# An issue planner with refitted estimates, an early ScalarE table load and unpaired squares in a hybrid SSD/S5 layer

## The chip, the cores and the metric
The kernel runs on one core of one Trainium2 chip. The metric is the device time of one execution in microseconds (us), the median of three runs. TensorE (PE) multiplies matrices, VectorE (DVE), ScalarE (ACT) and GpSimd (POOL) work element by element, SyncE (SP) issues the transfers between main memory and the on-chip buffers.

## What is computed
One inference step of one layer, for 1024 frames of a new stream and 32 frames of a running one, in fp32:

```
xn = RMSNorm(x);  P = xn @ W_in  -> [z | xBC | dt | u]        (1024 -> z 512, xBC 1024, dt 8, u 512)
SSD: causal conv + SiLU on xBC, chunked scan over 8 heads, + D*x, gated by SiLU(z), grouped RMSNorm
S5:  32 groups of 16 channels, 64 complex states each, Re(C h) + D*u, GELU, per-group GLU
h = x + RMSNorm([ssd | s5] @ W_out)
[g | v] = causal_dwconv3(RMSNorm(h) @ W_up)                   (1024 -> 2 x 2816)
y = h + RMSNorm((gelu(g) * v) @ W_down)
```
The new states and the last rows of the convolutions are outputs too.

## The kernel before
The 1056 frames lie along the columns of every tile, the channels along the 128 partitions, and are worked in chunks of 512, 272 and 272 columns (0, 1, 2). Each fp32 operand of a large product is split into a high and a low half, and `mm` (L479) runs three products for one: xh·wh, xl·wh, xh·wl. ScalarE makes the high halves (`act`, L535), VectorE the low ones by subtraction: xl at L1045 for the input, L1662 for the second norm, wl at L713 for each 128x1024 weight block (`raw` is the block as it landed). The weights go by in an order written out at L687 and following: 16 blocks of W_in, W_out for each chunk, W_up, and W_down.

The head: `prologue` (L1033) loads the eight 128-channel pieces of a chunk's x into tiles `xst`, makes xh and xl of each, and hands the piece to `flush` (L1023), which squares it in place on ScalarE. For chunk 0 the squares of the pieces named in `pairs` are added to the square before on GpSimd (L1029). `norm_cols` (L675) then sums over the channels with matmuls of one column (`onec`, a column of ones), four 128-frame blocks for each remaining square; `rsq` (L597) computes the inverse root of the sums, beginning with `nrt` (L603) on VectorE, and `spread` makes the scale of all frames (`rbc`) by way of the tiles `scr` (L639 to L647). Products are computed from the unscaled x and multiplied by rbc when they are taken out of PSUM, at L758 (uext) in the S5 part and at L1721 (fext) in the feed-forward part.

S5 runs eight times over four groups each. In a run TensorE multiplies `ug` by `GT` into PSUM; VectorE scans; GpSimd and VectorE write `hq` (L1164 to L1168); TensorE multiplies hq by `W`; ScalarE and VectorE make `ge` (a GELU) of that; TensorE multiplies ge by the weight `gluw`. Between these steps stand matmuls of the input projection.

After W_out the first norm's result is put on x at L1659 (tile `o`, from the product's scaled `oacc`, eight times for chunk 0). At the end of chunk 0's feed-forward part VectorE adds up its output in `acc` (L1891, L1896) while chunk 1's W_up products run; dl (L1771) is the low half of a W_down block.

The order is set by the class `Plan`. The program's instructions are recorded, their dependencies found (`read`), each given a duration and a latency (`cost`), and a list scheduler (`schedule`) goes forward and backward over them, `rounds` times, with priorities from the pass before; the shortest planned end wins, and `apply` fixes each engine's order to it. A successor on another engine is ready when its predecessor ends plus a fixed hand-over. SP's transfer issues are part of the same order.

Of the kernel before, what the change touches and what calls it, by code (L numbers as in the profile page):

```python
# [9 lines left out]
F32 = mybir.dt.float32  # L10
# [37 lines left out]
           run3=0.5, uload=6.619, swap_pool=1, z_s5=1, ssd0=13.784, ssd1=0.0, ssd2=2.778, gate0=76.032, glu0=0.384, glu1=2.807, abufs=2,   # L48
           cvat='run7', tcat=1, late_at=2, nsq=1, fg=(), fp=((1, 3), (1, 3), (3,)), fch=(0, (0, 1), 2), pfin=0, q0=0, q1=0, q2=0, nb=0, 
           hv=(), av=(3,), post0=0.802, dn_at=((3, 0), (3, 1)), ob_at=22, sa=2, sb=1, y5b=0, cvb=2.11, msb=(1, 1, 2, 2, 2), pch0=(3,),   # L50
           pch1=(3,), pch2=(3, 4), pf=0, pb=500, pg=0, pn=500, pr=0, pairs=(1, 2, 3, 5, 6), cf=4, cb=1, cg=0, cf2=2, cb2=(0, 1), cg2=0, 
           pgt=500, p5at=1, ng=0, n12=(2, 0), cho=2, dtlag=112.5, ng2=1, pairs2=(1, 2, 3, 5, 6, 7))
WIN, WOUT, WUP, WDN = 0, 16, 24, 68
TAU = [7, 6, 5, 4, 3, 2, 1, 0, 1, 2, 3, 4, 5, 6, 7, 8]
# [127 lines left out]
class Plan:  # L182
# [61 lines left out]
    def read(self):  # L244
# [18 lines left out]
        for q, i in enumerate(ins):  # L263
            ia, oa = aps(i.ins), aps(i.outs)
            self.cost(q, i, ia, oa)
            for _, g in ia:
                self.pre[q].update(k for k, h in w.get(g[0], ()) if self.meet(g, h))
            for _, g in oa:
                for d in (w, r):
                    self.pre[q].update(k for k, h in d.get(g[0], ()) if self.meet(g, h))  # L270
            for _, g in oa:
                for d in (w, r):
                    d[g[0]] = [(k, h) for k, h in d.get(g[0], ()) if not self.holds(g, h)]
                w[g[0]].append((q, g))
                use.setdefault(g[0], []).append(q)
            for _, g in ia:
                r.setdefault(g[0], []).append((q, g))
                use.setdefault(g[0], []).append(q)
            if type(i).__name__ == "InstMatmult":
                if i.start_tensor_calc and oa[0][1][0] in closed:  # L280
                    self.pre[q].add(closed[oa[0][1][0]])
                closed[oa[0][1][0]] = q
            self.pre[q].discard(q)
# [58 lines left out]
    def cost(self, q, i, ia, oa):  # L342
        self.eng[q] = e = str(i.engine).split(".")[-1]
        kind = type(i).__name__
        n = max(self.free(a) for a, _ in ia + oa)
        if kind == "InstDMACopy":
            self.bytes[q] = 4 * int(np.prod([m for _, m in ia[0][0].ap]))
            self.dur[q], self.lat[q] = 0.06, 2.0
            return
        if kind == "InstMatmult":  # L350
            n, m = (self.free(a) for a, _ in ia[:2])
            if ia[0][0].dtype == F32R:
                d = max(0.43 * n + 6, 107 if m > 64 else 54)
            elif i.is_transpose:
                d = 112
            else:
                d = 2 * max(0.85 * n, 108) if m > 64 else 0.85 * n
            self.dur[q], self.lat[q] = d * 1e-3, 0.07
            return
        big = [a for a, _ in ia if self.free(a) > 1]  # L360
        ps = any(g[0].startswith(("ms", "pm")) for _, g in ia)
        if kind == "InstActivation":
            self.fset[q] = str(i.func).split(".")[-1]
            d = 0.19 + 0.00085 * n + 0.08 * (len(ia) > len(big))
        elif e == "Pool":
            self.shared[q] = len(big) > 1
            d = 0.21 + 0.00165 * n if len(big) > 1 else 0.12 + 0.0009 * n
        else:
            self.shared[q] = not ps and n > 8
            d = 0.15 + (0.00105 if ps or len(big) > 1 else 0.00053) * n  # L370
        self.dur[q] = d

    def schedule(self, rank, pre, suc, forward=True, gate=None):
# [5 lines left out]
        order = {e: [] for e in engs}  # L379
        lock = wire = 0.0  # L380
        lanes, cur = [0.0] * DMA_LANES, None
        for q in range(n):
            if not left[q]:
                heappush(wait[self.eng[q]], (0.0, q))
        parked, todo = [], n
        while todo:
# [16 lines left out]
            if e == "Activation" and forward and not gate:  # L403
                need = [ACTSET.get(self.fset[q], cur) for _, q in avail[e]]
                k = min(range(len(need)), key=lambda k: (avail[e][k][0] + (4.0 if need[k] != cur else 0.0), avail[e][k][1]))
                q = avail[e].pop(k)[1]
                heapify(avail[e])
                if need[k] != cur:
                    cur = need[k]
                    t += 1.3  # L410
            else:
                q = heappop(avail[e])[1]
            start[q] = s = t
            order[e].append(q)
            if self.bytes[q]:
# [16 lines left out]
                    heappush(wait[self.eng[x]], (t, x))  # L432
                parked = []
            for x in suc[q]:
                v = free[e] if self.eng[x] == e and not self.bytes[q] else end[q] + 0.06
                if v > ready[x]:
                    ready[x] = v
                left[x] -= 1
                if not left[x]:
                    heappush(wait[self.eng[x]], (ready[x], x))  # L440
        return max(end), order, start, end

    def apply(self, rounds=3):
        self.read()
        self.buffers()
        best = self.schedule(list(range(len(self.ins))), self.pre, self.suc)
# [12 lines left out]
def body(tc, xT, wt, wdt, vec, cst, dtp, hist4, hist3, h0ssd, s5p, s5bc, s5d, glu, glub,  # L459
# [200 lines left out]

    onec = con.tile([128, 1], F32, name="onec")
    G.memset(onec, 1.0)
    ones_r = con.tile([128, 128], F32R, name="ones_r")
    G.tensor_copy(ones_r, onec.to_broadcast([128, 128]))
    ones = ones_r.bitcast(F32)
# [1280 lines left out]
```

## Time and profile before

| | us |
|---|---|
| median of 3 runs (lowest, highest) | 1297.89 (1296.71, 1302.05) |
| the profiled execution, its own time | 1294.34 |
| its span, first to last instruction | 1292.4 |
| TensorE busy | 1225.8 |
| VectorE busy | 1035.2 |
| ScalarE busy | 574.5 |
| GpSimd busy | 397.7 |

The profile is one execution. Busy time is per engine and over the span; the granted clock is TensorE's, as a share of 2.4 GHz, so 0.50 is 1.2 GHz. In a timeline the bracket behind an instruction is the idle time of its engine before it and what ended it.

### The profile page before, as it was taken

How to read it: one execution, taken by the hardware profiler on the slowest of the kernel's cores; microseconds unless marked ns; L12 is line 12 of the kernel's file. 1: busy time of each engine (PE TensorE's matmuls, PEld its weight loads, DVE VectorE, ACT ScalarE, POOL GpSimd, SP SyncE). 2: the span in 40 equal slices, each digit the busy share in tenths (PEclk: the TensorE clock that was granted, in tenths of full speed). 3: DMA queues.
4: the chain of work that ended last, by engine and by line, in shares of the span. 5: the costliest groups of instructions: out<-in, count | busy, mean ns of one | idle time of the engine just before them, and what ended most of it. 6: DMA issues, size and time to landing. Idle time of an engine off the chain costs nothing.

```text
span 1292.4 us, 20981 instructions
## 1 busy us (share of the span) xinstructions
PE 1225.8 (95%) x7880; PEld 1105.6 (86%) x7880; DVE 1035.2 (80%) x1781; ACT 574.5 (44%) x979; POOL 397.7 (31%) x577
## 2 busy tenths in 40 slices
PE   6879999999998999999999999998999999999995
PEld 5768888888877888878977888887999999999994
DVE  7898887988988998987688977679577777777777
ACT  7236466554555555543444433353523333333243
POOL 5364554544146433211345110015111111111113
PEclk8989999999998999999999999999999999999997
DMA  7133323233434423234433333222323332222212
GB/s 220 57 96 99 96 76 114 79 106 93 124 105 164 152 91 99 81 104 137 153 99 123 122 99 98 95 85 82 117 81 98 99 98 82 95 86 83 82 52 70
DMA packets 66901, 132.14 MB, mean 102 GB/s; under 512 B 13936, under 2 KB 34800, under 8 KB 66800
## 3 DMA queue, kind: packets, MB, share of 16 engines
q1 hardware_dynamic: 66800, 130.81, 32.2%
q8 instruction: 62, 1.02, 0.3%
q14 instruction: 39, 0.32, 0.1%
HBM read 111.69 MB, written 15.81 MB: 99 GB/s over the span
## 4 chain that ended last, share of the span: by engine, by line
PE 79%; DVE 10%; POOL 3%; issue 3%; DMA 2%; ACT 1%; SPq 1%; DVEq 0%; ACTq 0%; POOLq 0%
PE pm L479 70%; PE ms L479 9%; DVE wl L713 1%; POOL pacc L1666 1%; POOL o L1660 1%; DVE o L1659 1%; SPq L1122 1%; DMA xst<-xT 1%; DVE scr L647 1%; DVE scr L646 1%; POOL oacc L1628 1%; PE ms L483 1%; DVE pq L996 1%; POOL hq L1164 0%; DVE yr L1104 0%
## 5 line engine op out<-in xcount | busy, mean ns | idle before, releaser
L479 PE MATMUL pm<-xh,wh 128*128 128x272 f32 (+1 forms) x1616 | 532.1, 330 | 15.9 <-ACT wh L535 8.7
L479 PE MATMUL pm<-xh,wl 128*128 128x272 f32 (+1 forms) x1616 | 531.1, 329 | 7.4 <-DVE wl L713 7.3
L479 PE MATMUL pm<-xl,wh 128*128 128x272 f32 (+1 forms) x1616 | 529.8, 328 | 1.7 <-DVE xl L1045 1.7
L479 PEld LDWEIGHTS pm<-xh,wh 128*128 128x128 f32 x1616 | 309.9, 192 | 37.8 <-ACT wh L535 8.7
L479 PEld LDWEIGHTS pm<-xh,wl 128*128 128x128 f32 x1616 | 309.0, 191 | 30.8 <-DVE wl L713 9.1
L479 PEld LDWEIGHTS pm<-xl,wh 128*128 128x128 f32 x1616 | 309.9, 192 | 24.4 <-DVE xl L1045 3.0
L535 ACT ACTIVATE wh<-raw 128x1024 fp32r<-128x1024 f32 x120 | 126.9, 1057 | 177.5 <-PE pm L479 109.5
L713 DVE TENSOR_TENSOR wl<-raw,wh 128x1024 fp32r<-128x1024 f32 x120 | 154.9, 1291 | 26.6 <-ACT wh L535 26.1
L479 PE MATMUL pm<-al,dh 128*128 128x272 f32 (+1 forms) x528 | 171.4, 325 | 0.6 <-DVE al L1751 0.6
L479 PE MATMUL pm<-ah,dh 128*128 128x272 f32 (+1 forms) x528 | 171.7, 325 | 0.3 <-ACT ah L535 0.3
L479 PE MATMUL pm<-ah,dl 128*128 128x272 f32 (+1 forms) x528 | 170.8, 324 | 0.0
L1793 DVE TENSOR_TENSOR acc<-acc,pm 128x272 f32<-128x272 f32 (+1 forms) x235 | 121.1, 520 | 53.6 <-PE pm L479 52.5
L1738 DVE SCALAR_TENSOR_TENSOR ftmp<-fext,vec_t,ftmp 128x512 f32<-128x512 f32 (+1 forms) x176 | 143.1, 814 | 3.9 <-ACT ftmp L535 2.1
L1716 POOL COPY fext<-halo 128x2 f32<-128x2 f32 x88 | 33.6, 382 | 293.0 <-DVE ftmp L1738 271.5
L1721 DVE TENSOR_TENSOR fext<-pm,rbc 128x512 f32<-128x512 f32 (+2 forms) x132 | 67.5, 511 | 69.2 <-PE pm L479 65.8
L479 PEld LDWEIGHTS pm<-ah,dh 128*128 128x128 f32 x528 | 99.4, 188 | 8.6 <-ACT ah L535 0.7
L479 PEld LDWEIGHTS pm<-al,dh 128*128 128x128 f32 x528 | 99.3, 188 | 8.1 <-DVE al L1751 0.9
L479 PEld LDWEIGHTS pm<-ah,dl 128*128 128x128 f32 x528 | 99.2, 188 | 7.7 <-issue 0.3
L535 ACT ACTIVATE dh<-raw 128x1024 fp32r<-128x1024 f32 (+1 forms) x46 | 46.7, 1018 | 108.3 <-PE pm L479 96.8
L535 ACT ACTIVATE ftmp<-fext,vec_t 128x512 f32<-128x512 f32 (+1 forms) x88 | 72.3, 822 | 11.1 <-DVE fext L1721 5.7
L535 ACT ACTIVATE ftmp<-ftmp 128x512 f32<-128x512 f32 (+1 forms) x44 | 28.4, 644 | 87.0 <-DVE ftmp L1738 87.0
L1771 DVE TENSOR_TENSOR dl<-raw,dh 128x1024 fp32r<-128x1024 f32 (+1 forms) x46 | 55.9, 1216 | 13.6 <-ACT dh L535 13.6
(318 smaller groups left out, 1668.7 us busy)
## 6 DMA issues: line engine op xcount, KB each, us to landing
raw<-wt SPq DMA_DIRECT2D x164, 512.0 KB, 3.3
gluw<-glu SPq DMA_DIRECT2D x8, 512.0 KB, 3.4
xst<-xT SPq DMA_DIRECT2D x16, 136.0 KB, 3.3
pbd<-pbo SPq DMA_DIRECT2D x8, 272.0 KB, 2.6
xr<-xT SPq DMA_DIRECT2D x8, 272.0 KB, 3.2
pbi<-pbd SPq DMA_DIRECT2D x8, 272.0 KB, 3.5
yT<-acc SPq DMA_DIRECT2D x8, 272.0 KB, 2.3
ud<-uext SPq DMA_DIRECT2D x4, 528.0 KB, 4.0
```

The lines of the kernel that those rows point to most:

```text
L479: PE.matmul(out, lhsT, rhs, start=start, stop=stop, **kw)
L483: PE.transpose(out, in_, ident)
L535: S.activation(out, in_, func, bias=bias, scale=scale)
L646: e.tensor_scalar(hi[:L, o:o + L], ident[:L, :L], r[:L, i:i + 1], None, mult)
L647: last[0] = V.scalar_tensor_tensor(lo[:L, o:o + L], ident[:L, :L], r[:L, i:i + 1], hi[:L, o:o + L].bitcast(F32), mult, sub)
L713: V.tensor_tensor(lo, r, hi.bitcast(F32), sub)
L996: V.tensor_scalar(pq[lo:hi, a], src[lo:hi, :, o:o + 8], sg, None, mult)
L1716: G.tensor_copy(e[:, 0:2], halo[:, j, :])
L1721: V.tensor_tensor(e[:, 2 + o:2 + o + wp], ps[:, :wp], rbc[:, t0:t0 + wp], mult)
L1738: V.scalar_tensor_tensor(t, e[:, i:i + n], vc("fw", 3 * j + i), t, mult, add)
L1771: V.tensor_tensor(l, rr, h.bitcast(F32), sub)
L1793: V.tensor_tensor(a, a, ps[:, :w], add)
```

## The change
Three edits go in together. Lines of the new kernel lie 9 further down from L662 or so on, and 10 from L672 on (L479 is L488, L535 is L544, L713 is L723, L1045 is L1055, L1659 is L1669).

1. A one-element ScalarE activation (`warm`) is issued on `onec`. The table load that ScalarE needs ahead of its first activation is thereby free of the first transfer.
2. `pairs` is empty: chunk 0's eight squares all go to TensorE. GpSimd has five 128x512 additions less, TensorE 20 one-column matmuls more (32 for 12).
3. The planner's numbers: a transfer's issue takes 0.45 us for 0.06, its latency depends on its size; matmuls, strided operands, scans, per-partition scalars and GpSimd's one-input operations have new durations; the first ScalarE instruction carries a table load; a hand-over to another engine costs 0.6 us for 0.06; there are eight rounds for three. Reads of one PSUM tile by one engine keep the order in which they were written down.

```diff
-           pch1=(3,), pch2=(3, 4), pf=0, pb=500, pg=0, pn=500, pr=0, pairs=(1, 2, 3, 5, 6), cf=4, ...
+           pch1=(3,), pch2=(3, 4), pf=0, pb=500, pg=0, pn=500, pr=0, pairs=(), cf=4, ...
...
             for _, g in ia:
+                if g[0].startswith(("ms", "pm")):
+                    self.pre[q].update(k for k, h in r.get(g[0], ()) if self.eng[k] == self.eng[q])
                 r.setdefault(g[0], []).append((q, g))
...
-            self.dur[q], self.lat[q] = 0.06, 2.0
+            self.dur[q], self.lat[q] = 0.45, 1.7 + self.bytes[q] / 350e3
...
-                d = max(0.43 * n + 6, 107 if m > 64 else 54)
+                d = max(0.426 * n + 9, 107 if m > 64 else 54)
...
+        one = len(ia) - len(big)
+        far = any(a.ap[-1][1] > 1 and abs(a.ap[-1][0]) > 2 for a in big + [a for a, _ in oa])
...
-            d = 0.19 + 0.00085 * n + 0.08 * (len(ia) > len(big))
+            d = 0.19 + (0.00185 if far else 0.00085) * n + 0.09 * one
...
-            d = 0.21 + 0.00165 * n if len(big) > 1 else 0.12 + 0.0009 * n
+            d = 0.21 + 0.00165 * n if len(big) > 1 else 0.17 + 0.0009 * n
...
-            d = 0.15 + (0.00105 if ps or len(big) > 1 else 0.00053) * n
+            scan = getattr(i, "is_tensor_tensor_scan", False)
+            d = 0.15 + (0.0021 if scan else 0.0018 if far else 0.00105 if ps or len(big) > 1 else 0.00053) * n + 0.05 * one
...
+            if e == "Activation" and cold:
+                cold = False
+                t += 1.3
...
-                v = free[e] if self.eng[x] == e and not self.bytes[q] else end[q] + 0.06
+                v = free[e] if self.eng[x] == e and not self.bytes[q] else end[q] + 0.6
...
-    def apply(self, rounds=3):
+    def apply(self, rounds=8):
...
     G.memset(onec, 1.0)
+    act(con.tile([128, 1], F32, name="warm"), onec, AF.Silu)
```

The instructions are otherwise the same ones (ScalarE has 22 table loads for 18); their order moves on every engine and almost everywhere. Three places follow.

ScalarE at the start of the program, before:

```order
L535 ACT_TABLE_LOAD
L535 ACTIVATE xh_111<-xst,vec_t 128x512
L535 ACTIVATE xst<-xst 128x512
L535 ACTIVATE wh<-raw 128x1024
L535 ACTIVATE xh_111<-xst,vec_t 128x512 x3
L535 ACTIVATE xst<-xst 128x512
L535 ACTIVATE xh_111<-xst,vec_t 128x512 x2
```
and after:

```order
L544 ACT_TABLE_LOAD
L544 ACTIVATE warm<-onec 128x1
L544 ACTIVATE xh_113<-xst,vec_t 128x512
L544 ACTIVATE wh<-raw 128x1024
L544 ACTIVATE xh_113<-xst,vec_t 128x512
L544 ACTIVATE xst<-xst 128x512
L544 ACTIVATE xh_113<-xst,vec_t 128x512 x3
L544 ACTIVATE xst<-xst 128x512
L544 ACTIVATE xh_113<-xst,vec_t 128x512 x3
L544 ACTIVATE xst<-xst 128x512 x6
```
The first weight's high half stands ahead of the first square, and six of the eight squares now come in one row at the end of the chunk. TensorE's order follows: five of chunk 0's one-column matmuls stand among the first weight's products and 27 in one block behind them, where there were one and a block of eleven. On VectorE some 25 operations of the S5 parameters (L914 to L951, before L904 to L941) and one wl now stand ahead of chunk 0's nrt, among the xl of chunk 1; two of them stood there before.

TensorE in S5 run 2, from the last ug,GT matmuls on, before:

```order
L479 MATMUL ms_1535<-ug,GT 128x132 x2
L479 MATMUL pm<-xl_112,wh 128x512
L479 MATMUL pm<-xh_111,wl 128x512
L479 MATMUL pm<-xh_111,wh 128x512
L479 MATMUL pm<-xl_112,wh 128x512
L479 MATMUL pm<-xh_111,wl 128x512
L479 MATMUL pm<-xh_111,wh 128x512
L479 MATMUL pm<-xl_112,wh 128x512
L479 MATMUL pm<-xh_111,wl 128x512
```
and after:

```order
L488 MATMUL ms_1552<-ug,GT 128x132 x2
L488 MATMUL ms_1650<-ug,Tg 128x132
L488 MATMUL pm<-xl_114,wh 128x512
L488 MATMUL pm<-xh_113,wl 128x512
L488 MATMUL pm<-xh_113,wh 128x512
L488 MATMUL pm<-xl_114,wh 128x512
L488 MATMUL pm<-xh_113,wl 128x512
L488 MATMUL pm<-xh_113,wh 128x512
```
Before, the eight 512-column matmuls shown and 25 272-column ones of chunk 1 follow, then the first hq,W. After, there are 23 of 512 columns, two small ones and 22 of 272 columns ahead of it. The other runs move alike by less, or not at all.

VectorE at the end of chunk 0's feed-forward part, behind the last scr, before:

```order
L1738 SCALAR_TENSOR_TENSOR ftmp<-fext,vec_t,ftmp 128x546
L1721 TENSOR_TENSOR fext<-pm,rbc 128x272
L1771 TENSOR_TENSOR dl<-raw,dh 128x1024
L1891 TENSOR_TENSOR acc_4883<-acc_4883,sacc 128x1024
L1896 TENSOR_TENSOR acc_4883<-acc_4883,hr 128x512 x2
L1721 TENSOR_TENSOR fext<-pm,rbc 128x240
L1723 TENSOR_TENSOR fext<-pm,rbc 128x32
L1891 TENSOR_TENSOR acc_4883<-acc_4883,sacc 128x1024
L1738 SCALAR_TENSOR_TENSOR ftmp<-fext,vec_t,ftmp 128x546
L1721 TENSOR_TENSOR fext<-pm,rbc 128x272
L713 TENSOR_TENSOR wl<-raw,wh 128x1024
```
and after:

```order
L1731 TENSOR_TENSOR fext<-pm,rbc 128x272
L1731 TENSOR_TENSOR fext<-pm,rbc 128x240
L1733 TENSOR_TENSOR fext<-pm,rbc 128x32
L1781 TENSOR_TENSOR dl<-raw,dh 128x1024
L723 TENSOR_TENSOR wl<-raw,wh 128x1024
L1901 TENSOR_TENSOR acc_4900<-acc_4900,sacc 128x1024
L1906 TENSOR_TENSOR acc_4900<-acc_4900,hr 128x512 x2
L1748 SCALAR_TENSOR_TENSOR ftmp<-fext,vec_t,ftmp 128x546 x2
L1758 TENSOR_TENSOR ftmp<-ftmp 128x546
```
Both evacuations and the weight's low half (wl) moved ahead of the output's additions; four more evacuations follow what is shown, then the next wl, then the other L1901 and L1906. At the first post-norm (L1659, now L1669) one wl more stands ahead of the eight additions, and the next one stands behind all eight and four xl, where it stood behind seven of them.

## Rows read from the trace of the kernel before

**Rows 1.** The page, busy us of each engine, share of the span, instructions
```profile
PE 1225.8 (95%) x7880; PEld 1105.6 (86%) x7880; DVE 1035.2 (80%) x1781; ACT 574.5 (44%) x979; POOL 397.7 (31%) x577
```
**Rows 2.** Stretches: length, busy us (and instructions) of each engine, clock, DMA share, GB/s
```profile
32.00:64.00 32.00, 28.29 (x169) 24.83 (x168) 28.21 (x86) 8.01 (x15) 11.80 (x26) 0.95 0.17 56
64.00:97.00 33.00, 25.18 (x147) 21.85 (x146) 30.40 (x47) 11.15 (x26) 22.53 (x22) 0.84 0.35 96
...
1000.00:1260.00 260.00, 260.00 (x2075) 260.00 (x2074) 192.54 (x355) 90.53 (x129) 32.59 (x113) 1.00 0.26 84
```
**Rows 3.** TensorE's waits: for what, us in total, times, longest
```profile
PE pm L479 <- DVE wl L713: 7.3, 3, 4.2
PE ms L479 <- DVE scr L639: 5.2, 1, 5.2
PE ms L479 <- POOL hq L1168: 4.3, 3, 1.7
...
PE ms L479 <- issue: 3.7, 2, 1.9
...
PE ms L479 <- ACT ge L535: 1.9, 1, 1.9
```
**Rows 4.** Timeline of the head: start, length, engine, instruction, idle before it
```profile
4.24 1.28 ACT L535 ACT_TABLE_LOAD   x1 [4.24 <-DMA xst<-xT]
5.53 0.72 ACT L535 ACTIVATE xh<-xst,vec_t 128x512 fp32r<-128x512 f32 x1
6.29 0.75 DVE L1045 SCALAR_TENSOR_TENSOR xl<-xst,vec_t,xh 128x512 fp32r<-128x512 f32 x1 [3.14 <-ACT xh L535]
...
7.61 1.04 ACT L535 ACTIVATE wh<-raw 128x1024 fp32r<-128x1024 f32 x1
...
8.70 0.79 PE L479 MATMUL pm<-xh,wh 128*128 128x512 f32 x1 [8.70 <-ACT wh L535]
```
**Rows 5.** VectorE's timeline in the head
```profile
9.82 7.16 DVE L1045 SCALAR_TENSOR_TENSOR xl<-xst,vec_t,xh 128x512 fp32r<-128x512 f32 x6
...
24.48 0.16 DVE L603 TENSOR_SCALAR nrt<-ms 128x4 f32<-128x4 f32 x1 [1.23 <-PE ms L479]
```
**Rows 6.** GpSimd's timeline in the head
```profile
11.31 5.12 POOL L1029 TENSOR_TENSOR xst<-xst 128x512 f32<-128x512 f32 x3 [8.26 <-ACT xst L535]
...
17.01 2.96 POOL L1029 TENSOR_TENSOR xst<-xst 128x512 f32<-128x512 f32 x2
```
**Rows 7.** TensorE's timeline in the head: chunk 0's block of one-column matmuls
```profile
20.80 3.64 PE L479 MATMUL ms<-onec,xst 128*128 128x1 f32 x22
```
**Rows 8.** Two stretches at the lower clock, columns as in rows 2
```profile
22.00:28.80 6.80, 6.80 (x32) 6.80 (x33) 5.33 (x20) 5.87 (x14) 3.44 (x11) 0.50 0.54 145
...
899.20:906.00 6.80, 4.40 (x18) 4.11 (x19) 6.77 (x7) 0.75 (x2) 6.72 (x7) 0.50 0.23 86
```
**Rows 9.** TensorE's timeline in S5 run 2: two 512-column matmuls, the first hq
```profile
154.21 0.40 PE L479 MATMUL pm<-xl,wh 128*128 128x512 f32 x1
154.44 0.39 PE L479 MATMUL pm<-xh,wl 128*128 128x512 f32 x1
...
159.12 0.72 PE L479 MATMUL ms<-hq,W 128*128 128x132 f32 x4 [1.06 <-POOL hq L1168]
```
**Rows 10.** VectorE's timeline at the first post-norm
```profile
401.77 9.92 DVE L1659 SCALAR_TENSOR_TENSOR o<-o,vec_t,oacc 128x512 f32<-128x512 f32 x7 [1.22 <-ACT oacc L535]
411.61 2.28 DVE L713 TENSOR_TENSOR wl<-raw,wh 128x1024 fp32r<-128x1024 f32 x1
```
**Rows 11.** TensorE's timeline there: the two matmuls behind a pause
```profile
391.12 0.38 PE L479 MATMUL ms<-onec,oacc 128*128 128x1 f32 x2 [1.53 <-POOL oacc L1628]
...
413.94 0.39 PE L479 MATMUL pm<-xh,wl 128*128 128x272 f32 x1 [4.23 <-DVE wl L713]
```
**Rows 12.** VectorE's timeline at chunk 0's last norm
```profile
890.62 4.49 DVE L1896 TENSOR_TENSOR acc<-acc,hr 128x512 f32<-128x512 f32 x2
```
**Rows 13.** TensorE's timeline there: the matmul behind the long pause
```profile
900.63 0.57 PE L479 MATMUL pm<-xh,wh 128*128 128x272 f32 x1 [4.12 <-DVE fext L1721]
```

More of the change, by code (lines that the diff above doesn't have):

```diff
@@ L50 @@
            hv=(), av=(3,), post0=0.802, dn_at=((3, 0), (3, 1)), ob_at=22, sa=2, sb=1, y5b=0, cvb=2.11, msb=(1, 1, 2, 2, 2), pch0=(3,),
-           pch1=(3,), pch2=(3, 4), pf=0, pb=500, pg=0, pn=500, pr=0, pairs=(1, 2, 3, 5, 6), cf=4, cb=1, cg=0, cf2=2, cb2=(0, 1), cg2=0,
+           pch1=(3,), pch2=(3, 4), pf=0, pb=500, pg=0, pn=500, pr=0, pairs=(), cf=4, cb=1, cg=0, cf2=2, cb2=(0, 1), cg2=0,
            pgt=500, p5at=1, ng=0, n12=(2, 0), cho=2, dtlag=112.5, ng2=1, pairs2=(1, 2, 3, 5, 6, 7))
@@ L381, in schedule @@
         lanes, cur = [0.0] * DMA_LANES, None
+        cold = forward
         for q in range(n):
```

## The prediction
> **What bounds the kernel now.** I read the page's busy times first, then the table of stretches, then TensorE's waits, and only then the engines' own rows at the places where those waits lie. TensorE is busy 1225.8 us of a 1292.4 us span [rows 1]. The stretch from 1000 to 1260 us has no idle time at all; there 2075 matmuls take 260 us, so the usual 272-column matmul costs 0.125 us [rows 2]. None is removed by the change, so time can come only from TensorE's pauses and from stretches at the lower clock. The pauses of over 0.35 us, added up from TensorE's timeline, are 56.7 us, the first 8.7 of them the start and the last 5.2 the tail; the waits that matter below are those for VectorE's low weight halves (wl) 7.3, for GpSimd's hq 4.3, and 3.7 and 1.9 in front of the ge matmuls [rows 3]. From 32 to 97 us the picture is turned round: TensorE is busy 28.29 of 32 and 25.18 of 33 us, VectorE 28.21 and 30.40 [rows 2], so there VectorE sets the pace. The lower of the two clock levels, 1.2 GHz, is granted for instance from 22.0 to 28.8 and from 899.2 to 906.0, where the mean reads 0.50 [rows 8]; the first follows a run of one-column matmuls, the second a pause.
>
> **The head (0 to 97 us).** Four things change.
> The table load took 1.28 us after the first transfer had landed at 4.24; xh needs 0.72, wh 1.04, and wh began at 7.61 because a square stood before it [rows 4]. With the load done during the transfer and wh second in line, wh can begin between 4.96 and 6.6 and the first matmul come at 6.1 to 7.7 instead of 8.70. I take 7.1 (the weight's own landing, not in the rows, should come last): 1.6 us.
> The five additions on GpSimd go; they took 5.12 and 2.96 us [rows 6]. Beside them six xl took 7.16 us, 1.19 each, where one alone took 0.75 [rows 4, 5]. Eight times 0.44 gives VectorE 3.5 us back, in the stage that VectorE paces. The Trainium skill, "SBUF — State Buffer", section "SBUF: two separate sides", says that the port pair which VectorE and GpSimd share is an exclusive lock and the loser waits for the whole instruction. By that VectorE would get back up to the five additions' whole 8.1 us and the head's gain would be some 7 us; the xl rows show less than half of it, so the sum goes by the row.
> Twenty one-column matmuls are added, each two passes. Twenty-two passes took 3.64 us, 0.165 each, partly at the lower clock [rows 7, 8]. The order now has 27 in one block, 54 passes: 8.9 us, with bounds 6.0 (0.11, the full clock) and 11.9 (0.22, half). The block can start near 15 us, as chunk 0 is no longer held up by xl, so it ends at 21 to 27, near 24; the norm's first row (nrt) came at 24.48, after 1.23 us in which VectorE had waited for this sum [rows 5].
> VectorE now has some 25 S5 parameter operations and one wl ahead of nrt. At nrt's 0.16 us [rows 5] they are 4.0, the wl about 1.2. They fit into the 3.5 freed and the 1.23 of waiting with half a microsecond left over, and that work is then missing later, between 32 and 52, where VectorE is the bound. Queued behind them on VectorE are the norm, then the scr pieces that TensorE and the first evacuations wait for.
> What counts at 97 us is the VectorE work done: 3.5 + 1.2 + some of the earlier start, less up to 2 for a later norm: **+3 us**, bounds -3 (block at half clock, norm late) and +6.
>
> **S5 hand-overs (100 to 285 us).** Here the 0.6 us that the planner now puts on a hand-over shows most. In run 2, eight 512-column and 25 272-column matmuls stand between the last ug,GT and the first hq,W; a 512-column one takes 0.23 [rows 9], so the cover was 1.84 + 3.13 = 5.0 us and 1.06 was waited. Now 23 and 22 stand there: 5.3 + 2.8 = 8.0, over the 6.0 needed. By the same count run 5 goes from 5.0 to 8.3 (its wait was 1.48, a third of hq's 4.3), and ahead of ge, runs 2 and 4 go from 5.9 to 9.0 and from 7.1 to 9.05, where 1.86 and 1.80 were waited (both in the 3.7 of "issue") [rows 3, 9]. All four covered are 6.2 us; the margin in run 4 is 0.15 us only. The waits of run 7 on hq (the longest of the three, 1.7, cover 9.7 before and now) and run 1 on ge (1.9, cover now shorter by 2.2) stay or grow [rows 3]. **+5 us**, bounds +2 and +7. What waits in that chain is GpSimd and ScalarE work, and the new order has 22 table loads for 18, the added ones mostly here. At 1.28 each [rows 4] they are 5 us on an engine that is busy 44% [rows 1]. The Trainium skill, "ScalarE: Activation LUTs", section "What ACT_TABLE_LOAD costs", gives about 2.66 us for a switch, with a drain behind the load. In the head xh starts as the load ends (4.24 + 1.28 against 5.53). By the page run 4's and one other cover would be gone and this term about +2.
>
> **First post-norm (390 to 420 us).** Before, TensorE waited 1.53 for oacc and 4.23 for a wl that stood behind seven L1659 operations [rows 10, 11]. After, 66 matmuls (8.3 us) stand ahead of that onec,oacc, so the 1.53 goes. One more wl now stands ahead of the L1659s, but the next stands behind eight of them and four xl, twelve operations of 1.42 (9.92/7) or more: 17 to 21 us with its own 2.28 on top, of which TensorE has about 16 covered. A wait of 3 to 8 in place of 5.8: **-1 us**, bounds -4 and +3.
>
> **Chunk 0's last norm (886 to 906 us).** VectorE adds up sacc and hr there; one pair took 4.49 us [rows 12], and TensorE paused 4.12 for an evacuation [rows 13] and 0.97 for wl behind it, then ran 4.40 us of work at half clock, 2.2 lost [rows 8]. Now both evacuations, dl and one wl come before the first such group, so TensorE has two weights (12 us) instead of one in hand. But the next wl stands behind 1.2 + 4.5 of adding, three gating operations and four evacuations, 13 to 18 us in all: 1 to 5 us are waited there instead. Of 7.3 I take back **+3**, bounds -1 and +7.
>
> **Elsewhere** rows move everywhere. Stretches without idle time can only lose, the small pauses (dt, kd, hT, y, pacc, some 10 us together) can only shrink or wander: 0, bounds -4 and +4. The tail's order is nearly the same; its 5.2 us wait for scr stays.
>
> **Sum.** 3 + 5 - 1 + 3 = 10 us. The profiled execution took 1294.34, so 1284 by that; the median of the three runs, 1297.89, lies 3.55 higher, so I predict **1288**. If the bounds go independently their sum spreads by some 8 us either way.
>
> **Rivals.**
> (a) VectorE refills the gaps: wherever TensorE is no longer stopped, it reaches VectorE's next backlog sooner, and the waits come back as wl and fext waits behind the L1659 and L1896 groups. For: VectorE is busy 80% [rows 1] and the large waits after 400 are its [rows 11, 13]. Against: the S5 waits are for GpSimd and ScalarE, which are busy 31% and 44% [rows 1], so VectorE need not come next. Then the head's and half the S5's gain remain as slack and 0 to 5 us are won: about 1295.
> (b) Slower, by a late norm: the block of 27 one-column matmuls runs at half clock (11.9 for 8.9), starts late because it waits for ScalarE's six squares behind it, and the parameter operations with the wl push nrt further, for the whole S5 set-up is queued behind the scr pieces. It decides if nrt comes after 33 us: then the stage that VectorE paces moves by 8 or more, and with a post-norm wait of 8 (-4) and nothing won at 890 the S5's +5 doesn't repay it: 8 + 4 - 5 = 7 slower, about 1305.
> (c) The slack pays everywhere: between 15 and 1270 us the timeline has some 42 us of pauses, and some 31 us of matmul work in stretches at half clock, which costs 15. If the better-fitting durations and the hand-over take two fifths of that, 23 to 25 us go: about 1273. For: the waits removed in S5 are of just this kind. Against: the largest ones are long VectorE groups, which the planner knew before.
> That the order doesn't move as the costs say can be ruled out by the rows of the order; that the table load still waits for the transfer would cost 1.3 at the head and little at the end.
>
> **Chances.** Forecast (1282 to 1293) 0.47; (a) 0.20; (b) 0.14; (c) 0.19. About 0.5%, 6.5 us, is what a measurement of this kernel can tell from no change. Below 1291.4 lie nine tenths of the forecast, (c) and a little of (a): 0.64 faster. Within lie the rest of the forecast and most of (a): 0.22. Above 1304.4: 0.14. The range 1272 to 1304 leaves out half of (c) below and about a tenth of the chance above.
>
> **What would show it.** The first matmul near 7.1 and nrt between 21 and 27; xl of chunk 0 at about 0.75; a granted clock of 0.5 or 1.0 in the onec block; no wait for hq or ge in runs 2, 4 and 5; the wait near 405 to 420 at 3 to 8 us; the 4.12 pause near 897 gone and a shorter one for wl a weight later; the stretches 500 to 600 and 1000 to 1260 still without idle time. I am wrong if nrt comes after 33, if the post-norm wait is over 8, or if idle time appears in stretches that have none.

## The result, and the profile after

The changed kernel takes 1267.32 us (median of 4 runs, 1267.05 to 1267.70) where the kernel before takes 1297.85 in the same session: a ratio of 0.9759, 95% interval 0.9737 to 0.9781, so 30.5 us less. 1288 was predicted, with a range of 1272 to 1304. The direction was right, the size a third of what came, and the range ended 5 us too high. Of a_jitter's four executions below, the profiled one was a slow one (1727 us at a mean granted clock of 0.65), so its time is the median of the other three and its trace isn't used.

The profiled execution has a span of 1265.3 us, 27.1 less. The page of the kernel after, busy time of each engine:

```profile
PE 1225.4 (97%) x7920; PEld 1107.6 (88%) x7920; DVE 1034.4 (82%) x1781; ACT 580.2 (46%) x984; POOL 413.4 (33%) x572
```

TensorE is busy as long as before [rows 1], although 40 passes were added in the head. Less time at half clock gives back some of that: the stretches in which the granted clock read 0.50 between the start and the tail add up to 34.1 us, where they were 37.5. Where the rest comes from isn't shown. Its idle time fell from 1292.4 - 1225.8 = 66.6 us to 39.9, by 26.7, and that is nearly the whole difference of the spans. Where the idle time went, three stretches of the kernel after, and under them the same stretches of the kernel before (length, then busy us and count of TensorE's matmuls, its weight loads, VectorE, ScalarE, GpSimd; clock, DMA share, GB/s):

```profile
0.00:97.00 97.00, 86.12 (x513) 75.02 (x513) 79.64 (x183) 48.32 (x97) 50.88 (x85) 0.91 0.43 132
97.00:290.00 193.00, 191.49 (x1334) 175.89 (x1334) 177.25 (x276) 112.98 (x255) 96.48 (x99) 1.00 0.39 106
640.00:1000.00 360.00, 356.55 (x2131) 320.24 (x2130) 281.60 (x459) 148.47 (x216) 94.50 (x156) 0.99 0.31 103
```
```profile
0.00:97.00 97.00, 74.34 (x400) 64.01 (x401) 81.51 (x174) 43.25 (x87) 51.53 (x86) 0.89 0.41 124
97.00:290.00 193.00, 181.83 (x1262) 166.40 (x1260) 161.63 (x267) 108.89 (x246) 94.24 (x99) 0.99 0.33 95
640.00:1000.00 360.00, 350.98 (x2046) 310.40 (x2045) 276.46 (x456) 144.51 (x215) 89.68 (x151) 0.99 0.32 102
```

11.8 us of idle time are gone up to 97 us, 9.7 in the S5 stretch, 5.6 between 640 and 1000; 290 to 640 us gave 0.8, and behind 1000 about 1 was lost (the tail's wait for scr grew from 5.2 to 6.5). The stretches are cut by time, so the changed kernel is further on in the program at the end of each. Of the head's 11.8 the 40 added passes take 4.5 at the 0.112 a pass of the pairs near 376 us, at the full clock, and 6.4 at the 0.16 of the block in the head.

TensorE's waits after, to be laid beside [rows 3]:

```profile
PE pm L488 <- ACT wh L544: 7.2, 2, 6.7
PE ms L488 <- DVE scr L648: 6.5, 1, 6.5
PE pm L488 <- DVE wl L723: 4.3, 3, 2.3
PE ms L488 <- ACT E L544: 4.2, 1, 4.2
PE pm L488 <- DVE fext L1731: 2.7, 1, 2.7
```

Neither hq nor ge is in the list any more, and two waits near 80 us of the kernel before are gone too:

```profile
PE pm L479 <- DVE uext L758: 3.1, 1, 3.1
PE ms L479 <- POOL gz L1095: 3.0, 1, 3.0
```

### The profile page after: what moved, and what is told of

Same layout as the page of the kernel before. It is cut to its first block, busy times and chain, and to the rows that moved or that the text cites. A ratio compares the mean times of both kernels' runs of the same rounds, so it can differ in the third digit from the quotient of the medians.

```text
span 1265.3 us, 21067 instructions
## 1 busy us (share of the span) xinstructions
PE 1225.4 (97%) x7920; PEld 1107.6 (88%) x7920; DVE 1034.4 (82%) x1781; ACT 580.2 (46%) x984; POOL 413.4 (33%) x572
## 4 chain that ended last, share of the span: by engine, by line
PE 87%; DVE 9%; issue 2%; POOL 1%; DMA 0%; ACT 0%; SPq 0%; DVEq 0%; POOLq 0%; ACTq 0%
PE pm L488 77%; PE ms L488 10%; DVE o L1669 1%; DVE wl L723 1%; PE ms L492 1%; DVE xl L1672 1%; POOL pacc L1676 0%; DVE acc L1901 0%; DVE acc L1903 0%; DVE ftmp L1748 0%; DVE uext L768 0%; DVE R L1172 0%; DVE y5s L1215 0%; DMA raw<-wt 0%; DVE acc L1803 0%
## 5 line engine op out<-in xcount | busy, mean ns | idle before, releaser
L488 PE MATMUL pm<-xh,wh 128*128 128x272 f32 (+1 forms) x1616 | 530.2, 329 | 9.9 <-ACT wh L544 7.2
L488 PE MATMUL pm<-xh,wl 128*128 128x272 f32 (+1 forms) x1616 | 527.7, 329 | 4.5 <-DVE wl L723 4.3
L488 PE MATMUL pm<-xl,wh 128*128 128x272 f32 (+1 forms) x1616 | 528.9, 328 | 0.0
L488 PEld LDWEIGHTS pm<-xh,wh 128*128 128x128 f32 x1616 | 308.1, 191 | 32.1 <-ACT wh L544 7.7
L488 PEld LDWEIGHTS pm<-xh,wl 128*128 128x128 f32 x1616 | 306.4, 190 | 27.6 <-DVE wl L723 5.8
L488 PEld LDWEIGHTS pm<-xl,wh 128*128 128x128 f32 x1616 | 308.1, 191 | 22.2 <-issue 0.9
L544 ACT ACTIVATE wh<-raw 128x1024 fp32r<-128x1024 f32 x120 | 126.8, 1057 | 167.7 <-PE pm L488 133.1
L488 PE MATMUL pm<-al,dh 128*128 128x272 f32 (+1 forms) x528 | 170.2, 324 | 0.0
L488 PE MATMUL pm<-ah,dh 128*128 128x272 f32 (+1 forms) x528 | 170.2, 325 | 0.0
L488 PE MATMUL pm<-ah,dl 128*128 128x272 f32 (+1 forms) x528 | 168.9, 324 | 0.0
L723 DVE TENSOR_TENSOR wl<-raw,wh 128x1024 fp32r<-128x1024 f32 x120 | 154.5, 1287 | 11.9 <-ACT wh L544 11.2
L1726 POOL COPY fext<-halo 128x2 f32<-128x2 f32 x88 | 42.8, 486 | 302.4 <-DVE ftmp L1748 281.1
L544 ACT ACTIVATE ftmp<-fext,vec_t 128x512 f32<-128x512 f32 (+1 forms) x88 | 72.3, 824 | 82.7 <-DVE fext L1733 45.0
L488 PEld LDWEIGHTS pm<-ah,dh 128*128 128x128 f32 x528 | 99.3, 188 | 7.7 <-issue 0.2
L488 PEld LDWEIGHTS pm<-al,dh 128*128 128x128 f32 x528 | 99.2, 188 | 7.3
L488 PEld LDWEIGHTS pm<-ah,dl 128*128 128x128 f32 x528 | 98.7, 188 | 8.0 <-issue 0.3
L544 ACT ACTIVATE dh<-raw 128x1024 fp32r<-128x1024 f32 (+1 forms) x46 | 46.7, 1019 | 82.3 <-PE pm L488 65.5
L544 ACT ACTIVATE ftmp<-ftmp 128x512 f32<-128x512 f32 (+1 forms) x44 | 28.2, 641 | 74.9 <-DVE ftmp L1748 74.8
```

The lines of the kernel that those rows point to most:

```text
L488: PE.matmul(out, lhsT, rhs, start=start, stop=stop, **kw)
L544: S.activation(out, in_, func, bias=bias, scale=scale)
L723: V.tensor_tensor(lo, r, hi.bitcast(F32), sub)
L1726: G.tensor_copy(e[:, 0:2], halo[:, j, :])
```

## The experiments

Each kernel's time is the median of its runs, beside runs of the kernel before on the same chip (1296 to 1300 in every session). The next column is when TensorE's first product of a weight starts, the last three are its busy time in three stretches. A star marks kernels with the 40 added passes in the first.

| kernel | what it is | us | first product | 0-97 | 97-290 | 640-1000 |
|---|---|---|---|---|---|---|
| before | | 1297.9 | 8.7 | 74.3 | 181.8 | 351.0 |
| b_warmpairs | before + early table load + unpaired squares | 1296.9 | 24.5 | 81.0* | 184.7 | 351.7 |
| b_dur | before + durations | 1306.7 | 15.3 | 70.0 | 183.2 | 346.8 |
| b_handover | before + hand-over 0.6 | 1285.6 | 13.6 | 71.6 | 188.1 | 356.4 |
| b_handur | before + both | 1279.7 | 13.7 | 74.2 | 188.8 | 356.8 |
| after | | 1267.3 | 6.7 | 86.1* | 191.5 | 356.6 |
| a_handover006 | after, hand-over 0.06 | 1301.7 | 25.5 | 78.8* | 182.4 | 346.7 |
| a_handover03 | 0.3 | 1289.4 | 25.3 | 79.8* | 189.0 | 352.7 |
| a_handover05 | 0.5 | 1279.9 | 7.2 | 81.2* | 192.7 | 352.8 |
| a_handover07 | 0.7 | 1278.7 | 25.3 | 81.6* | 191.4 | 351.8 |
| a_handover10 | 1.0 | 1294.2 | 25.4 | 81.2* | 187.6 | 352.1 |
| a_ho_pe | 0.6 towards TensorE only | 1289.9 | 25.5 | 80.4* | 189.1 | 350.5 |
| a_ho_notpe | 0.6 everywhere else only | 1286.9 | 9.4 | 79.4* | 191.4 | 354.0 |
| a_olddur | after, old durations | 1280.9 | 25.6 | 81.7* | 186.7 | 357.7 |
| a_pairs | after, squares paired | 1277.9 | 13.8 | 75.3 | 190.5 | 356.1 |
| a_nowarm | after, no early load | 1277.1 | 9.6 | 80.6* | 189.9 | 356.5 |
| a_rounds3 | after, three rounds | 1269.0 | 6.6 | 84.9* | 192.4 | 356.8 |
| a_jitter | after, meaningless change | 1276.0 | | | | |
| a_jitter2 | after, meaningless change | 1272.9 | 7.1 | 84.0* | 191.5 | 355.9 |
| a_jitter3 | after, meaningless change | 1267.2 | 7.0 | 83.8* | 191.6 | 356.9 |

### Which part carries it: hand-over or durations

Theory H put the gain on the hand-over's slack, D on the refitted durations, P on the head's edits.

```diff
-                v = free[e] if self.eng[x] == e and not self.bytes[q] else end[q] + 0.06
+                v = free[e] if self.eng[x] == e and not self.bytes[q] else end[q] + 0.6
```

b_handover puts this line alone into the kernel before (with the rule on PSUM reads).

> The kernel before with the planner's hand-over at 0.6 us for 0.06 alone (and the rule that keeps reads of one PSUM tile in their written order, without which this order isn't possible; that rule alone leaves before's order as it was). Theory H, the hand-over's slack is what pays: most of the 30.5 us gained by the whole change, 15 to 25, is here: 1273 to 1283, the waits for hq and ge between 100 and 285 us gone. Theory D, the refitted durations pay: within 5 us of before, 1293 to 1300. Theory P, the head (early table load, no additions on GpSimd) pays: within 5 us of before too, and the head's waits as before.

1285.58 us, ratio 0.9905 (0.9869 to 0.9941): 11 us of the 30, less than H wanted. Its own stretches show where:

```profile
0.00:97.00 97.00, 71.62 (x393) 61.75 (x394) 80.25 (x179) 42.81 (x86) 47.40 (x83) 0.89 0.40 126
97.00:290.00 193.00, 188.09 (x1338) 174.17 (x1337) 180.03 (x277) 115.28 (x262) 106.53 (x103) 0.99 0.34 96
640.00:1000.00 360.00, 356.38 (x2090) 317.03 (x2089) 278.98 (x466) 146.70 (x218) 95.66 (x153) 0.99 0.32 103
```

In S5 it has 6.3 us less idle time than before and from 640 to 1000 5.4, but the head is 2.7 worse: its first product starts at 13.63 us, 4.9 later than before. No wait for hq is left; one for ge (2.6) and the one for uext (4.0) are:

```profile
PE pm L481 <- DVE uext L760: 4.0, 1, 4.0
PE ms L481 <- DVE ge L1195: 2.6, 1, 2.6
```

a_handover006 takes the same line back out of the changed kernel.

> The changed kernel with the hand-over put back to 0.06 us. H: most of the gain is lost, 1283 to 1293, and waits for hq and ge of 1 us and more come back between 100 and 285 us. D: within 5 us of the changed kernel, 1264 to 1272. P: the same as D.

1301.73, ratio to before 1.0041 (1.0022 to 1.0060): everything is lost, and 4 to 5 us more, beyond what H gave. The waits are back by name:

```profile
PE ms L488 <- POOL gz L1105: 3.5, 2, 3.1
...
PE pm L488 <- DVE uext L768: 3.3, 1, 3.3
...
PE ms L488 <- POOL hq L1178: 2.6, 3, 1.7
...
PE ms L488 <- ACT ge L544: 1.2, 1, 1.2
```

D falls with this run. The durations were taken out of the changed kernel (a_olddur) and put alone into the one before (b_dur), as the diff of the change has them:

> The changed kernel with all the planner's durations and the transfer latency as they were, hand-over 0.6 us kept. D: most of the gain is lost, 1283 to 1293. H: 0 to 6 us lost, 1267 to 1273. P: the same as H.

1280.94, 13.6 lost, between what H and what D gave.

> The kernel before with the refitted durations and transfer latency alone (hand-over 0.06 us; the rule on reads of one PSUM tile comes along, since this order isn't possible without it). Theory A, the parts add up: the durations were worth 13.6 us inside the changed kernel, so 1280 to 1286 here. Theory J, durations pay only together with the hand-over, since without slack a well-known chain is planned to the last tenth and any delay is waited for: 1293 to 1303, and the waits for gz and uext near 80 us (3.0 and 3.1 before) still there.

1306.72, ratio 1.0074 (1.0047 to 1.0100): 9 us slower than before, outside what either theory gave. The refitted numbers alone leave the gz and uext waits where they were:

```profile
PE ms L484 <- POOL gz L1100: 3.6, 2, 3.3
...
PE pm L484 <- DVE uext L763: 3.3, 1, 3.3
```

b_handur joins hand-over and durations and leaves the rest of the change out.

> The kernel before with hand-over and durations together, without the early table load, the unpaired squares, the cold first activation and the five more rounds. A: 1296.7 - 11.1 - 13.6 = 1272 (1269 to 1275), with the S5 stretch as much ahead as in either. J: at least as good, 1268 to 1275; the waits for gz and uext near 80 us gone, which neither part alone removes. If the head's edits carry more than the 10.6 us that pairs showed, 1278 or more.

1279.74, ratio 0.9869 (0.9836 to 0.9903): 18 of the 30 us are here. Neither A's nor J's number came; 1278 or more had been the sign of head edits that carry more, which the next section doesn't bear out as it stands. Slack is worth 27 us beside the new durations (b_dur to b_handur) and 34 in the changed kernel (a_handover006 to after), but 11 beside the old ones: the parts don't add up. The durations cost 9 us without slack, and with it they are worth 6 (the intervals of the two ratios overlap) or 13.6. These last are of the size that a meaningless reshuffle of the order makes, as shown below, so what the durations are worth by themselves isn't shown.

### The head's edits

```diff
-    act(con.tile([128, 1], F32, name="warm"), onec, AF.Silu)
```
and, in another kernel, `pairs=(1, 2, 3, 5, 6)` again:

> The changed kernel without the early table load (the planner still counts a table load ahead of ScalarE's first instruction). J and A: the first matmul comes 1.3 to 2 us later, 1268 to 1271. If the first weight's start is what the head's gain hangs on, 1272 to 1278 and a lead at 97 us that is smaller by as much.

> The changed kernel with chunk 0's squares paired on GpSimd again (five 128x512 additions there, 20 one-column matmuls fewer on TensorE). P: chunk 0's xl take about 1.2 us beside the additions again, the first scaled outputs come later, and 3 to 8 us are lost: 1270 to 1276. H and D: within 3 us of the changed kernel, since the 40 passes that go (6 us of TensorE in a stretch where it has time to spare) and the additions that come nearly cancel: 1264 to 1270.

1277.10 and 1277.92: each seems worth 10 us, far more than a first matmul 3 us later (9.63 us in a_nowarm) can explain, and more than any of their theories gave but the last one of a_nowarm. In the kernel before, both together:

> The kernel before with the early table load and the unpaired squares alone, planner untouched. A: pairs alone were worth 10.6 us inside the changed kernel, so 1283 to 1288. J: the head is VectorE's and its lead is lost at the waits near 80 us, so 1292 to 1300; the first matmul near 7 us instead of 8.7 all the same.

1296.91, ratio 1.0000 (0.9983 to 1.0017): nothing. The early start didn't come as expected, though: the first matmul, at 6.32 us, is one of the squares', which TensorE now takes first, and the first product comes at 24.46 us.

```profile
6.32 0.56 PE L479 MATMUL ms<-onec,xst 128*128 128x1 f32 x2 [6.32 <-ACT xst L535]
...
24.46 0.77 PE L479 MATMUL pm<-xh,wh 128*128 128x512 f32 x1
```

So the run shows what the edits give in the order that the old planner makes of them. Either they pay only under the new planner, or the 10 us aren't theirs. Since any number that the planner is given moves rows everywhere, three kernels changed one by an amount that means nothing:

```diff
-                d = max(0.426 * n + 9, 107 if m > 64 else 54)
+                d = max(0.426 * n + 10, 107 if m > 64 else 54)
```
```diff
-            self.dur[q], self.lat[q] = 0.45, 1.7 + self.bytes[q] / 350e3
+            self.dur[q], self.lat[q] = 0.45, 1.75 + self.bytes[q] / 350e3
```
```diff
-            d = 0.21 + 0.00165 * n if len(big) > 1 else 0.17 + 0.0009 * n
+            d = 0.22 + 0.00165 * n if len(big) > 1 else 0.17 + 0.0009 * n
```

> The changed kernel with 1 ns more for every fp32r matmul in the planner's durations (0.426 n + 10 for + 9), nothing else. Theory C, chance of the order: differences of 10 us between variants come from any reshuffle, so 1272 to 1282. Theory O, the head's edits own their 10 us: within 4 us of the changed kernel, 1263 to 1271.

> The changed kernel with 0.05 us more for every transfer's latency in the planner. Few rows move. C: 1267 to 1280. O: within 3 us of the changed kernel.

> The changed kernel with 0.01 us more for GpSimd's two-input operations in the planner's durations. Spread as seen: 1267 to 1281, more likely above the changed kernel than below it, if that is the best of several such orders.

1276.01, 1272.88 and 1267.22. A reshuffle alone is worth 0 to 9 us, none of the three is faster than the changed kernel, and two are slower. a_nowarm and a_pairs, 10 and 11 us slower, lie only 1 to 2 us above the slowest of them, and a hand-over of 0.5 or 0.7 for 0.6 (below) costs 13 and 11. So by their times alone the 10 us can't be put down to the table load or the squares.

Two readings of the traces speak for a part of it all the same. In the three kernels with paired squares and 0.6 the first product comes at 13.6 to 13.8 us (in a_pairs the first weight's high half stands behind all eight xh and four squares); in those with unpaired squares, 0.6 and the new durations it comes at 6.6 to 9.6. And by the matmuls done at 97 us (an estimate, explained further down) the changed kernel, a_rounds3, a_jitter2 and a_jitter3 are 6.5 to 9.0 us ahead of the kernel before, a_pairs 5.9, a_nowarm and b_handur 3.1. That would be a few us for the head's edits. But a_handover05 and a_handover07, which have both edits, lead by 2.8 and 5.5 only, so it isn't shown.

```diff
-    def apply(self, rounds=8):
+    def apply(self, rounds=3):
```

> The changed kernel with three rounds of the planner instead of eight. If the extra rounds found what made the whole change better than its parts: 1272 to 1280. If the parts do (hand-over, durations, both head edits together): within 3 us of the changed kernel's 1267, since few rows of the order differ.

1269.01, ratio 0.9789 (0.9775 to 0.9804) where the changed kernel has 0.9759: the extra rounds bring 2 to 4 us, which is no more than a reshuffle makes.

### Slack or a truer number

> The changed kernel with a hand-over of 0.3 us. A gain that grows with the slack: between the 1301.7 of 0.06 and the 1279 of 0.5 and 0.7, so 1283 to 1296. A threshold near what GpSimd and ScalarE chains really lose per step: within 1275 to 1283 already.

> The changed kernel with a hand-over of 0.5 us. Broad optimum: 1264 to 1274. A lucky value: 1275 to 1290.

> The changed kernel with a hand-over of 0.7 us. Broad optimum: 1264 to 1274. A lucky value, or a fall towards the 1294 of 1.0 us: 1275 to 1290.

> The changed kernel with a hand-over of 1.0 us. Theory S, the number is slack, and more of it buys more cover: 1260 to 1270, all waits for hq and ge between 100 and 285 us gone. Theory M, the number should match what a hand-over takes on this chip: the further off the worse, 1272 to 1285.

1289.36, 1279.94, 1278.65 and 1294.16 us, with 1301.73 for 0.06 and 1267.32 for 0.6. Allowing 9 us for the reshuffle, the time falls up to about 0.5, lies low to 0.7 and has risen again at 1.0. 0.5 and 0.7 came where a lucky value at 0.6 had been expected to put them, not at the 1264 to 1274 of a broad optimum: 0.6 is 11 to 13 us better than both, and both have the head's edits. Theory S (more slack, more cover) fails at 1.0; theory M, as I put it, fails too, since of the numbers tried the one that matches the chip is the worst. What a hand-over takes is seen where nothing else is in the way. In the head of the kernel after, wh ends at 5.56 + 1.06 = 6.62 and the matmul that waits for it starts at 6.67, 0.05 later (from VectorE's wl, ending at 401.39 + 2.29, to the matmul at 403.73 it is 0.05 too):

```profile
0.73 1.28 ACT L544 ACT_TABLE_LOAD   x1 [0.73 <-PEq L1947]
...
4.31 0.72 ACT L544 ACTIVATE xh<-xst,vec_t 128x512 fp32r<-128x512 f32 x1 [2.09 <-DMA xst<-xT]
5.56 1.06 ACT L544 ACTIVATE wh<-raw 128x1024 fp32r<-128x1024 f32 x1 [0.53 <-DMA raw<-wt]
...
6.67 0.79 PE L488 MATMUL pm<-xh,wh 128*128 128x512 f32 x1 [6.67 <-ACT wh L544]
```

So 0.06 is about what these hand-overs take, and 0.6 is slack. That it works as a reserve against what the planner's durations don't hold is my reading, and wasn't tested. With 1.0 hardly an hq or ge wait is left (0.9 for ge); instead there are 4.8 us of waits for xl and 2.6 for xh at the post-norm, 3.4 for dt near 96 us and 5.8 for fext near 899 us. Why the planner's order breaks there wasn't tested.

Which hand-overs need it was asked with the slack on those towards TensorE alone, and on all others alone:

```diff
-                v = free[e] if self.eng[x] == e and not self.bytes[q] else end[q] + 0.6
+                v = free[e] if self.eng[x] == e and not self.bytes[q] else end[q] + (0.6 if self.eng[x if forward else q] == "PE" else 0.06)
```

> The changed kernel with 0.6 us on hand-overs to TensorE alone and 0.06 on all others. If slack pays just where TensorE waits: 1267 to 1273. If it pays along the chains between the other engines (PSUM to VectorE, GpSimd, ScalarE and back, four to six hand-overs from a ug,GT to its hq and from an hq to its ge): 1280 to 1300, with waits for hq and ge back.

> The other half: 0.6 us on all hand-overs but those to TensorE, 0.06 on these. By the first theory of the run before it 1285 to 1302, near the kernel with 0.06 everywhere (1301.7); by the second 1267 to 1278.

1289.92 and 1286.86: 12 and 15 us below the 1301.7 without any slack. The first lies in the second theory's range, the second in the first's, so neither theory holds for both: both halves are needed. The 3 us between them are less than a reshuffle makes.

## Why the prediction was right or wrong

**Where the miss lies.** To set the terms of the sum beside the result I counted the matmuls that each trace shows done by a given time, the squares' own left out, at their full-clock lengths (0.125 us for 272 columns, 0.227 for 512, 0.112 for the small ones). By this estimate the changed kernel is 1.4 us behind the kernel before at 75 us, 9 ahead at 97, 22 at 290, 21 at 640 and 27.7 at 1000, which fits the 27.1 between the spans. The head gave 9 for a forecast of +3 (upper bound 6), S5 13 for +5 (upper bound 7), the post-norm's stretch -1 for -1, and 640 to 1000 us 6.6 for +3 and 0. (The 56.7 us of pauses in the prediction are all pauses; those of over 0.35 us are 54.4, which changes none of its terms.)

**The head's first half was right in its rows.** First matmul 7.1 forecast, 6.67 came; the block of 54 passes 8.9 forecast, 8.65 came, partly at half clock; nrt between 21 and 27, 25.11 came. Chunk 0's xl were forecast at 0.75 and took 2.73/4 = 0.68. TensorE's, VectorE's and the clock's rows of the kernel after:

```profile
16.42 8.65 PE L488 MATMUL ms<-onec,xst 128*128 128x1 f32 x54
```
```profile
7.79 2.73 DVE L1055 SCALAR_TENSOR_TENSOR xl<-xst,vec_t,xh 128x512 fp32r<-128x512 f32 x4
...
25.11 0.16 DVE L612 TENSOR_SCALAR nrt<-ms 128x4 f32<-128x4 f32 x1 [2.76 <-PE ms L488]
```
```profile
18.30:28.50 10.20, 10.20 (x51) 10.01 (x51) 6.74 (x21) 6.24 (x15) 5.86 (x14) 0.56 0.64 172
```

The step that failed is the sum behind them. It took VectorE's freed time for the gain at 97 us and put the waits for gz and uext at nothing, without asking whether the order would keep them. VectorE did get its time back (58.0 us busy up to 75 us for 61.7), and TensorE has 4.5 us less idle time by then, but that goes to the added passes, so there is no gain yet. It comes between 75 and 97 us, where these two waits are gone and with them a stretch at half clock; before, and after:

```profile
75.00:97.00 22.00, 14.19 (x78) 11.85 (x78) 19.82 (x28) 7.35 (x16) 13.52 (x12) 0.77 0.29 77
```
```profile
75.00:97.00 22.00, 21.44 (x161) 17.81 (x160) 21.63 (x29) 10.01 (x24) 19.16 (x17) 1.00 0.38 109
```

Hand-over or durations alone leave one or both of the waits (uext 4.0 in b_handover; gz 3.6 and uext 3.3 in b_dur). How much of the 9 us is owed to the head's edits stays open, as said above.

**S5: the step that failed is that the need was held fixed.** The cover was counted in the new order, and the time that hq and ge need was taken from the trace before. By that the waits of run 7 on hq and run 1 on ge had to stay. They went, because the need is made by the same order. What ended run 7's wait was GpSimd's last copy into hq; before, rh stood between the scan R (VectorE, ending at 273.42) and GpSimd's half of hq, and xw and y between that half and the copies:

```profile
275.42 1.81 POOL L1164 TENSOR_TENSOR hq<-R,TS 128x528 f32<-128x528 f32 x1
277.18 1.51 POOL L1356 TENSOR_TENSOR xw<-xdt,wend 128x512 f32<-128x512 f32 x1
278.66 2.02 POOL L1391 TENSOR_TENSOR y<-xb,vec_t 128x512 f32<-128x512 f32 x1
280.62 0.70 POOL L1167 COPY fin<-hq 128x16 f32<-128x16 f32 x1
281.38 0.20 POOL L1168 COPY hq<-sml 128x8 f32<-128x8 f32 x1
```
```profile
281.63 0.72 PE L479 MATMUL ms<-hq,W 128*128 128x132 f32 x4 [1.72 <-POOL hq L1168]
```

and after (the scan ends at 252.19) its half stands right behind the scan and only rh in between, so that hq is whole 5.3 us behind the scan where it took 8.2, and TensorE takes it without waiting:

```profile
252.36 1.85 POOL L1174 TENSOR_TENSOR hq<-R,TS 128x528 f32<-128x528 f32 x1 [6.92 <-DVE R L1172]
254.15 2.40 POOL L1359 TENSOR_TENSOR rh<-dtah,cst_t 128x1024 fp32r<-128x1024 f32 x1
256.50 0.68 POOL L1177 COPY fin<-hq 128x16 f32<-128x16 f32 x1
257.24 0.20 POOL L1178 COPY hq<-sml 128x8 f32<-128x8 f32 x1
```
```profile
258.30 0.61 PE L488 MATMUL ms<-hq,W 128*128 128x132 f32 x4
```

Run 1's wait of 1.9 was for ScalarE, whose reading of the first ge products stood behind a Tg that its transfer held up until 141.44 us; after, Tg runs at 124.76, before those products begin at 127.08.

The four waits that I counted (6.2 us) went as forecast; with the others 9.7 us of idle time went between 97 and 290 us, and a stretch of 3.4 us at half clock near 114 us went as well. The reading that the added table loads lie mostly in S5 was wrong: the trace has 6 of them there for 5, the other three in the head and behind 290 us, none stands near run 4's ge, and the two near run 2's (142.05 and 147.96 us) left no wait. The Trainium skill, "ScalarE: Activation LUTs", section "What ACT_TABLE_LOAD costs", gives a drain of about 1380 ns beside a load's 1283. No such gap shows here: with a load right ahead of run 1's ge, the next activation starts 0.01 us behind the load's end.

```profile
121.14 1.28 ACT L544 ACT_TABLE_LOAD   x1
122.43 0.65 ACT L544 ACTIVATE ge<-ge 128x528 f32<-128x528 f32 x1
```

**The post-norm was right in size, with luck.** A wait of 3 to 8 us for wl in place of 5.8 was forecast; 4.20, 0.55 and 0.70 came, for E, wh and wl. Only the last is the wait that was reasoned out, behind L1669 and L1672 on VectorE. The longest is for E on ScalarE, behind activations that waited for a transfer (2.10) and for GpSimd's part of o (0.42).

```profile
401.06 1.98 PE L488 MATMUL ms<-cst_t,dta 128*64 128x128 f32 x16 [4.20 <-ACT E L544]
```

**The last norm was right in size, and the wait's name was wrong.** 1 to 5 us were forecast a weight later, for wl; 2.70 came, for an evacuation behind the gating operations, in place of 4.12 and 0.97 [rows 13]:

```profile
879.61 0.47 PE L488 MATMUL pm<-xh,wh 128*128 128x272 f32 x1 [2.70 <-DVE fext L1731]
```

**"Elsewhere 0" was too low, inside its bounds of 4.** From 640 to 1000 us 5.6 us of idle time went, about 2.4 of them the last norm's, the rest small waits for pacc, al, ah and scr between 650 and 702. Busy time there is 351.0 before, 346.7 and 346.8 in the two kernels with the new durations and 0.06, and 351.8 to 357.7 in all with 0.5 or more on every hand-over.

**The rivals.** (c), the slack paying everywhere, was nearest in kind and had a chance of 0.19; it gave 1273, still 6 us too slow. (a) and (b) didn't happen: no new VectorE backlog took the place of the removed waits, and nrt came at 25, not after 33. What no rival held is that the order itself carries a luck of up to 9 us: the range was made of known terms only, so its low end at 1272 lay above what three of five orders made by nearly the same numbers reach (1267.3, 1267.2, 1269.0, 1272.9, 1276.0).

What is shown: hand-over slack and durations together give 18 us, and the slack is needed (taking it away costs 27 and 34 us). What stays open is what the durations give by themselves, and how the last 12 split into the head's edits and the luck of the order, since no pair of kernels differs in these edits and keeps the order of the rest.

## What to carry to other kernels

A list scheduler that planned with the hand-over that the chip takes left waits at gz, uext, hq and ge, most likely because it puts each dependent so close that every duration that runs long is waited for. Slack on every hand-over, more than the chip takes and less than 1 us here, removed most of them; refitted durations without it did not. Measure what a meaningless change of the planner's numbers does before crediting an edit: here it was up to 9 us, nearly as much as each of two edits seemed to be worth. And look at what order an isolating experiment makes: the head's edits alone were tried in an order that held the first product back to 24 us. When waits are counted against a new order, count the waiting chain in the new order too.

## What the runs showed of the hardware

The same VectorE instruction took very different times, with different work of GpSimd beside it. The two additions of hr took 4.47 us in one place, while GpSimd ran two-input additions, and 1.29 fourteen microseconds later, while it copied two columns (VectorE's and GpSimd's timelines of the kernel after):

```profile
868.36 4.47 DVE L1906 TENSOR_TENSOR acc<-acc,hr 128x512 f32<-128x512 f32 x2
...
882.53 1.29 DVE L1906 TENSOR_TENSOR acc<-acc,hr 128x512 f32<-128x512 f32 x2
```
```profile
867.20 3.38 POOL L1901 TENSOR_TENSOR acc<-acc,sacc 128x1024 f32<-128x1024 f32 x1
870.65 3.33 POOL L1906 TENSOR_TENSOR acc<-acc,hr 128x512 f32<-128x512 f32 x2
...
882.48 0.18 POOL L1743 COPY o<-fext 128x2 f32<-128x2 f32 x1
```

With one input it was alike: the table TC took 1.17 us beside GpSimd's two-input operations in the kernel before and 0.43 with GpSimd waiting (idle from 71.2 to 74.5 us) in the kernel after.

```profile
80.94 1.17 DVE L899 TENSOR_SCALAR TC<-yr 128x528 f32<-128x528 f32 x1
```
```profile
72.16 0.43 DVE L909 TENSOR_SCALAR TC<-yr 128x528 f32<-128x528 f32 x1
```

The granted clock fell within a block of one-column matmuls here, as it had behind one in [rows 8]: in the 54 passes from 16.42 on it still read 1.00 up to 18.3 us, and 0.56 was the mean from there to 28.5, though TensorE was busy all the time.
